# A decoder layer on one core: low parts of expert weights on VectorE, remainder rows by halves, second pass of two norms on VectorE

## The chip, the cores and the metric

The kernel runs on one core of one Trainium2 chip. The metric is device time in microseconds (us), the median of several executions. The engines are TensorE (PE; its weight loads are listed apart as PEld), VectorE (DVE), ScalarE (ACT), GpSimd (POOL) and SyncE (SP, which here only issues DMAs).

## The reference

One decoder layer over 1024 tokens of 1024 channels. Its first sublayer (sparse attention and RWKV-7 side by side) and the second (cross-attention) come before the part that is changed. The change touches the norm after the second sublayer, the mixture of experts, and the last norm:

```python
y = memory_cross_attention(x, mem, xq_w[l], xk_w[l], xv_w[l], xo_w[l])
x = layer_norm(DN_ALPHA * x + y, ln2_g[l], ln2_b[l])
y = grouped_moe(x, router_w, router_bias, moe_w_gate[l], moe_w_up[l], moe_w_down[l])
x = layer_norm(DN_ALPHA * x + y, ln3_g[l], ln3_b[l])
```

`grouped_moe` sends each token to 2 of 16 experts; an expert is `(silu(x @ w_gate) * (x @ w_up)) @ w_down` with a hidden width of 512, and its results are weighted and summed per token. With the reference's inputs, and the reference's own routing evaluated on them, the 16 experts get 123, 122, 118, 141, 118, 132, 142, 134, 129, 111, 138, 108, 127, 122, 123 and 160 tokens.

## The kernel before

Every f32 operand of a large product is split into a high part (rounded to fp32r by ScalarE) and a low part (the difference). A product is three matmuls, high by high, high by low, low by high (`Ctx.mm3`, lines 35 to 37).

**Second norm and routing.** `Xattn.out` makes one tile of 128 tokens at a time: TensorE's two halves, VectorE's residual add (line 1236), then `Norm.__call__`. A norm takes moments on VectorE (978, 979), `rs = (var + eps) ** -0.5` in two GpSimd instructions on 128x1 (980, 981), the first pass `(x - mean) * g` on VectorE (987), and the second pass `x * rs + b`, either as one VectorE instruction (992) or as a ScalarE multiply and a GpSimd add (989, 990). The list given as `pool_adds` says which tiles take the second way; the count starts at 1, so that `LN2P` of 0 to 7 means tiles 0 to 6. `Router.tile` then transposes the tile, forms logits, and after tiles 3, 6 and 7 `Router.route` finds experts and slots on VectorE (1338, 1341) and GpSimd scatters (row, gate) records into two lists in DRAM (1407). The first expert's tokens are picked by matmuls with a selection matrix (1417).

**Experts.** Each expert has room for 128 tokens (`CAP`, the "main" rows); the eight fullest, with expert 0 first, get 64 more (`REM`, the "remainder"). `rows` reads 128 list records, adds both lists, and makes two row numbers on GpSimd: the token to gather, and the row to add the result to, which for an empty slot is one of 128 spare rows behind the 1024. `gather` fetches rows of the normed x by an indirect DMA from GpSimd's queue (1551). For a remainder the 64 records are read twice, into both halves of the partitions, all 128 partitions gather whole rows, and half of every transpose is then dropped. High and low part of the remainder share one stationary operand of 128 columns, so that its results come out in two halves, both added by one indirect DMA each.

Weights come in pieces of 128x4x512 (six per expert); `parts` makes high and low of a piece in `CUT` = 4 steps: ScalarE casts (1528) and the difference is taken by GpSimd for the steps in `LOPOOL`, by VectorE otherwise (1529). `result` scales a result on ScalarE (1627) and adds its rows to `accd` in DRAM by an indirect DMA with accumulation (1632); each of these waits for the landing of the one before.

**End.** Before the last two experts are added, `tiles` loads `accd` tile by tile and norms it (`BYACT`: moments on ScalarE, 972 to 974; `ADDV`: second pass on VectorE, else ScalarE and GpSimd), and stores it. For the last two experts (`late`) the affected rows are gathered again, their results added (1629), normed, and scattered to the output (1635). `rest` handles experts with more than their room in a loop, which with these inputs runs no time.

The order of instructions on each engine is set when the program is built, by a scheduler over the whole program; engines issue in that order.

Of the kernel before, what the change touches and what calls it, by code (L numbers as in the profile page):

```python
# [7 lines left out]
F32 = mybir.dt.float32  # L8
F32R = mybir.dt.float32r
I32 = mybir.dt.int32  # L10
# [5 lines left out]
T, D = 1024, 1024  # L16
# [924 lines left out]

ALPHA = 2 ** 0.25
LN1P = ()
LN2P = (0, 1, 2, 3, 4, 5, 6, 7)
LN2A = ()
SQB = 2
EARLY = 4
# [291 lines left out]


NE, FF = 16, 512
CAP, REM = 128, 64
NREM = 8
FIXED = 1
# [1 line left out]
NSLOT = NE * REG  # L1246
NBLK = 15
LOOK = 4
BYACT, ADDV = (2, 3, 4, 5, 6), (0, 3, 5, 7)
NLAG = 1  # L1250
KINDS = ("raw", "hi", "lo")
NLST = 2
GROUPS = (4, 7, 8)
FIRST = (14, 6, 6, 6, 6, 6, 6, 7)
HOLD = 4
CUT, LOPOOL = 4, (2,)
LATE = 2


def host_consts5():  # L1260
    i = np.arange(128)
    rows = np.zeros((128, 8, 2, 4), np.float32)
    rows[:, :, :, 0] = (np.arange(8)[None, :] * 128 + i[:, None])[:, :, None]
    rows[:, :, :, 1] = 1
    e = np.arange(16)
    dum = (T + i).astype(np.float32)
    return {"c_upper": (i[:, None] < i[None, :]).astype(np.float32),
            "c_ones": np.ones((128, 128), np.float32),
            "c_e16": np.tile(np.concatenate([e - 16, REG * e]).astype(np.float32), (128, 1)),
            "c_rows": rows, "c_dum": np.stack([dum, -dum], 1),  # L1270
            "c_ii": np.tile(np.eye(64, dtype=np.float32), (2, 1)),
            "c_iota": np.tile(np.arange(128, dtype=np.float32), (128, 1)),
            "c_thr": np.tile((128 * np.arange(7)).astype(np.float32), (1, 16, 1)),
            "c_key": np.where(e < FIXED, 1e6 - e, 15 - e).astype(np.float32)[None],
            "c_er": np.stack([e, REG * e]).astype(np.float32)[None],
            "c_blk0": np.arange(NBLK).astype(np.float32)[None]}
# [195 lines left out]
class Experts:  # L1472
    def __init__(self, k, cst, p, pw, dp, router, x2d, out):
        self.out, self.held = out, 0
        self.k, self.r, self.x2d, self.ident = k, router, x2d, cst["ident"]
        nc = k.nc
        self.acc = dp.tile([T + 128, D], F32, name="accd")
        self.dum, self.ii = p.tile([128, 2], F32, name="dum"), pw.tile([128, 64], F32, name="ii")
        nc.sync.dma_start(self.dum, k.a["c_dum"])
        nc.sync.dma_start(self.ii, k.a["c_ii"])  # L1480
        nc.sync.dma_start(self.acc[T:T + 128, :].rearrange("p (a b) -> p a b", a=8), router.z[:, :128].unsqueeze(1).to_broadcast([128, 8, 128]))

        self.pre, self.at, self.done, self.seq = [], 0, [], []
        for n in range(NE + 1):
            self.seq += [(e, i) for e, i in ((n, 0), (n, 1), (n - 1, 4), (n - 1, 5), (n, 2), (n, 3)) if 0 <= e < NE]
        self.n, self.slots = {n: 0 for n in KINDS}, {n: [] for n in KINDS}
# [45 lines left out]
    def rows(self, pl, s0, tag, twice=False):  # L1532

        nc = self.k.nc
        l = pl.tile([128, NLST, 4], F32, tag="l" + tag, bufs=2, name="el")
        for i in range(NLST):
            src = self.r.lst[i][bass.ds(s0, 64 if twice else 128), :]
            nc.sync.dma_start(l[:, i, :], src.unsqueeze(0).to_broadcast([2, 64, 4]) if twice else src)
        f = pl.tile([128, 5], F32, tag="f" + tag, bufs=3, name="ef")
        ix = pl.tile([128, 2], I32, tag="ix" + tag, bufs=3, name="eix")  # L1540
        for i in range(1, NLST):
            nc.gpsimd.tensor_tensor(f[:, 0:4], l[:, 0] if i == 1 else f[:, 0:4], l[:, i], ALU.add)
        nc.gpsimd.tensor_copy(ix[:, 0:1], f[:, 0:1])
        nc.gpsimd.tensor_scalar(f[:, 4:5], f[:, 1:2], self.dum[:, 1:2], self.dum[:, 0:1], ALU.mult, ALU.add)
        nc.gpsimd.tensor_tensor(f[:, 4:5], f[:, 4:5], f[:, 0:1], ALU.add)
        nc.gpsimd.tensor_copy(ix[:, 1:2], f[:, 4:5])
        return ix, f[:, 2:3]

    def gather(self, px, ix, tag, src=None):
        xg = px.tile([128, D], F32, tag="xg" + tag, bufs=2 if tag == "m" else 1, name="exg")  # L1550
        self.k.nc.gpsimd.indirect_dma_start(out=xg, out_offset=None, in_=self.x2d if src is None else src, in_offset=bass.IndirectOffsetOnAxis(ap=ix[:, 0:1], axis=0))
        return xg

# [10 lines left out]
    def expert(self, px, ps, w, main, rem, first=None, late=False):  # L1564
# [14 lines left out]
        nc.vector.scalar_tensor_tensor(th, th, 1.0, o, ALU.add, ALU.mult)  # L1579
        if rem:  # L1580
            xr = px.tile([128, 8, 128], F32R, tag="exr", bufs=1, name="exr")
            for q in range(2):
                tp = self.turned(ps, rem[2], q).rearrange("p (c t) -> p c t", c=4)
                k.split(tp[:, :, 0:64], xr[:, 4 * q:4 * q + 4, 0:64], xr[:, 4 * q:4 * q + 4, 64:128])
            gr = px.tile([128, 2, 512], F32, tag="gr", bufs=1, name="egr")

        def more(i):
# [30 lines left out]
        def result(tag, x, mm):  # L1618
# [10 lines left out]
                    nc.vector.scalar_tensor_tensor(z[:, ds], o, x[1], z[:, ds], ALU.mult, ALU.add)  # L1629
            for r in ([slice(0, 128)] if tag == "m" else [slice(0, 64), slice(64, 128)]):  # L1630
                ix = x[0][0:r.stop - r.start, 1:2]
                nc.gpsimd.indirect_dma_start(out=self.acc, out_offset=bass.IndirectOffsetOnAxis(ap=ix, axis=0), in_=y[r, :], in_offset=None, compute_op=ALU.add)
            if late:
                self.ln(z)
                nc.gpsimd.indirect_dma_start(out=self.out, out_offset=bass.IndirectOffsetOnAxis(ap=x[0][:, 1:2], axis=0), in_=z, in_offset=None, bounds_check=T - 1, oob_is_err=False)
# [277 lines left out]
```

## Time and profile before

| | us |
|---|---|
| three runs | 1892.65, 1894.74, 1884.31 (median 1892.65) |
| profiled execution, its own time | 1896.58 |
| its span, first to last instruction | 1894.70 |
| mean granted TensorE clock | 0.959 |

The profile is of one execution, whose time lies 1.9 us above its span and 3.9 us above the median of the runs. Busy time is what an engine's instructions cover; a wait names what ended an engine's idle time. Times in the trace count from the start of the span.

### The profile page before, as it was taken

What the parts mean: (1) busy time and instruction counts of PE and PEld (TensorE: products, weight loads), DVE (VectorE), ACT (ScalarE), POOL (GpSimd) and SP (SyncE); (2) the same over time, 40 slices, a digit from 0 to 9 for tenths busy, and PEclk for the clock granted to TensorE, in tenths of its full rate; (3) what the DMA queues carried; (4) which work ended last, traced back from release to release, by engine and by line L of the source; (5) the groups of instructions that cost most, each with busy time, mean ns of one, the idle gap of its engine ahead of it and who ended that gap; (6) DMA issues with size and microseconds to landing.
All of it is one profiled execution on the core that took longest, in us unless ns stands there. A gap on an engine that the chain in (4) does not pass through costs nothing. (4 is left out here: it accounts for less than half of the span.)

```text
span 1894.7 us, 27396 instructions
## 1 busy us (share of the span) xinstructions
PE 1759.3 (93%) x9158; PEld 1433.4 (76%) x9158; DVE 1321.1 (70%) x2767; ACT 858.6 (45%) x1775; POOL 698.1 (37%) x780
## 2 busy tenths in 40 slices
PE   8999999999999899999999789999998999999991
PEld 6877777777687787888887577878787888877871
DVE  3225876888777621498987575546987788989876
ACT  4223313434332222298887441024414666667662
POOL 1123202221221121175747122100346576656556
PEclk9999989999999899999999899999989999999995
DMA  7363434444432226812101765133325999899984
GB/s 232 110 186 105 118 142 124 135 128 121 108 111 87 67 89 198 255 43 75 46 8 36 226 211 172 34 97 123 117 107 172 332 325 309 278 294 302 332 269 152
DMA packets 246143, 301.98 MB, mean 159 GB/s; under 512 B 54653, under 2 KB 142741, under 8 KB 245488
## 3 DMA queue, kind: packets, MB, share of 16 engines
q1 hardware_dynamic: 238016, 273.59, 44.4%
q0 software_dynamic: 7984, 26.62, 5.7%
q8 instruction: 73, 1.20, 0.3%
q14 instruction: 70, 0.57, 0.1%
HBM read 234.05 MB, written 70.98 MB: 161 GB/s over the span
## 5 line engine op out<-in xcount | busy, mean ns | idle before, releaser
L1529 DVE TENSOR_TENSOR wlo<-wraw,whi 128x512 fp32r<-128x512 f32 x288 | 281.1, 1026 | 26.1 <-ACT whi L1528 25.7
L35 PE MATMUL acc<-xh,wh 128*128 128x512 f32 (+1 forms) x656 | 273.6, 417 | 5.9 <-ACT wh L117 3.0
L36 PE MATMUL acc<-xl,wh 128*128 128x512 f32 (+1 forms) x656 | 267.1, 408 | 0.0
L37 PE MATMUL acc<-xh,wl 128*128 128x512 f32 (+1 forms) x656 | 266.6, 408 | 0.2 <-POOL wl L118 0.2
L1528 ACT CAST whi<-wraw 128x512 fp32r<-128x512 f32 x384 | 207.8, 623 | 35.4 <-PE eacc L1591 10.2
L118 POOL TENSOR_TENSOR wl<-wraw,wh 128x1024 fp32r<-128x1024 f32 (+1 forms) x41 | 100.8, 2459 | 308.6 <-ACT wh L117 259.2
L35 PEld LDWEIGHTS acc<-xh,wh 128*128 128x128 f32 (+1 forms) x656 | 125.1, 191 | 45.3 <-issue 8.0
L1529 POOL TENSOR_TENSOR wlo<-wraw,whi 128x512 fp32r<-128x512 f32 x96 | 138.8, 1482 | 46.4 <-ACT whi L1528 40.5
L37 PEld LDWEIGHTS acc<-xh,wl 128*128 128x128 f32 (+1 forms) x656 | 124.6, 190 | 33.7 <-issue 5.2
L36 PEld LDWEIGHTS acc<-xl,wh 128*128 128x128 f32 (+1 forms) x656 | 125.0, 191 | 29.8 <-issue 3.1
L851 DVE TENSOR_TENSOR tinv<-xinv,ln 128x248 f32<-128x248 f32 (+30 forms) x248 | 89.3, 360 | 40.6 <-DMA ln<-ld 15.6
L475 ACT ACTIVATE pp<-pp,nm 128x640 f32<-128x640 f32 (+7 forms) x128 | 94.3, 740 | 9.3 <-DVE nm L474 8.1
L28 DVE TENSOR_TENSOR pl<-ptp,ph 128x512 fp32r<-128x512 f32 x132 | 87.4, 685 | 12.0 <-ACT ph L28 11.3
L36 PE MATMUL eacc<-wlo,exh 128*128 128x512 f32 x240 | 94.2, 392 | 0.2 <-DVE wlo L1529 0.2
L35 PE MATMUL eacc<-whi,exh 128*128 128x512 f32 x240 | 94.2, 393 | 0.0
L37 PE MATMUL eacc<-whi,exl 128*128 128x512 f32 x240 | 94.2, 392 | 0.0
L480 POOL TENSOR_SCALAR pp<-pp,wgt 128x640 f32<-128x640 f32 (+7 forms) x128 | 88.4, 711 | 0.6
L852 DVE TENSOR_TENSOR xinv<-xinv,tinv 128x248 f32<-128x248 f32 (+30 forms) x248 | 84.0, 339 | 5.9
L980 POOL TENSOR_SCALAR lnrs<-lnmv 128x1 f32<-128x1 f32 x21 | 19.7, 936 | 180.5 <-DVE lnmv L979 172.6
L28 ACT CAST ph<-ptp 128x512 fp32r<-128x512 f32 x132 | 73.8, 583 | 16.9 <-PE ptp L534 16.1
L534 PE MATMUL ptp<-ident,pp 128*128 128x128 f32 x528 | 79.2, 276 | 0.4 <-DVE pl L28 0.2
L909 ACT COPY state<-rseq 64x64 f32<-64x64 f32 x128 | 26.8, 209 | 116.4 <-PE rseq L905 97.5
(502 smaller groups left out, 4542.9 us busy)
## 6 DMA issues: line engine op xcount, KB each, us to landing
wraw<-in_moe_w_up SPq DMA_DIRECT2D x32, 1024.0 KB
wraw<-in_moe_w_gate SPq DMA_DIRECT2D x32, 1024.0 KB
wraw<-in_moe_w_down SPq DMA_DIRECT2D x32, 1024.0 KB
wraw<-in_w_in SPq DMA_DIRECT2D x40, 512.0 KB
sm<-ev SPq DMA_DIRECT2D x32, 256.0 KB
sr<-ev SPq DMA_DIRECT2D x28, 256.0 KB
skew<-skew SPq DMA_DIRECT2D x1, 4608.0 KB
xraw<-in_x SPq DMA_DIRECT2D x8, 512.0 KB
```

What stands on the lines that cost most here:

```text
L28: x = nc.scalar.copy(hi, src), (nc.gpsimd if by_pool else nc.vector).tensor_tensor(lo, src, hi.bitcast(F32), ALU.subtract)
L35: nc.tensor.matmul(out, ah, bh, start=start, stop=False)
L36: nc.tensor.matmul(out, ah, bl, start=False, stop=False)
L37: nc.tensor.matmul(out, al, bh, start=False, stop=stop)
L118: nc.gpsimd.tensor_tensor(wl, raw, wh.bitcast(F32), ALU.subtract)
L475: nc.scalar.activation(pt[:, :n], pt[:, :n], AF.Exp, bias=nm, scale=-1.0, accum_out=sums[:, 0, i:i + 1])
L480: nc.gpsimd.tensor_scalar(st[br, i][:, :n], st[br, i][:, :n], w[:, 0, i:i + 1], 1.0, ALU.mult, ALU.mult)
L534: nc.tensor.transpose(tp[:, 128 * i:128 * i + 128], st[br, i][:, c0:c0 + 128], ident)
L851: nc.vector.tensor_tensor(tmp[:, :, :w], x[:, :, j:j + 1].to_broadcast([128, 8, w]), ln[:, j:j + 1, j + 1:].to_broadcast([128, 8, w]), ALU ...
L852: nc.vector.tensor_tensor(x[:, :, j + 1:], x[:, :, j + 1:], tmp[:, :, :w], ALU.subtract)
L1528: nc.scalar.copy(hi[:, cs], raw[:, cs])
L1529: (nc.gpsimd if i in LOPOOL else nc.vector).tensor_tensor(lo[:, cs], raw[:, cs], hi[:, cs].bitcast(F32), ALU.subtract)
```

## The change

Five things, all from the second norm on. (1) `LOPOOL` becomes empty: VectorE makes all low parts of the expert weights. (2) `LN2P` becomes empty and `ADDV` all eight tiles: the second pass of the second and last norm is VectorE's everywhere. (3) A remainder is gathered by halves: x is seen as 2048 half rows, the lower 64 partitions fetch the first half of their row (number 2r) and the upper 64 the second (2r + 1), one GpSimd instruction more makes the number, and four transposes and one split take the place of eight and two. (4) The adding DMA gets a bound, so that rows of empty slots are not written. (5) The row numbers lie in the same tile as the records, of which there are six per kind instead of three.

```diff
-LN2P = (0, 1, 2, 3, 4, 5, 6, 7)
+LN2P = ()
+NROWS = 6
-BYACT, ADDV = (2, 3, 4, 5, 6), (0, 3, 5, 7)
+BYACT, ADDV = (2, 3, 4, 5, 6), (0, 1, 2, 3, 4, 5, 6, 7)
-CUT, LOPOOL = 4, (2,)
+CUT, LOPOOL = 4, ()
-            "c_rows": rows, "c_dum": np.stack([dum, -dum], 1),
+            "c_rows": rows, "c_dum": np.stack([dum, -dum, (i >= 64).astype(np.float32)], 1),
...
-        f = pl.tile([128, 5], F32, tag="f" + tag, bufs=3, name="ef")
-        ix = pl.tile([128, 2], I32, tag="ix" + tag, bufs=3, name="eix")
+        f = pl.tile([128, 8], F32, tag="f" + tag, bufs=NROWS, name="ef")
+        ix = f[:, 6:8].bitcast(I32)
...
-        nc.gpsimd.tensor_copy(ix[:, 0:1], f[:, 0:1])
+        if twice:
+            nc.gpsimd.tensor_scalar(f[:, 5:6], f[:, 0:1], 2.0, self.dum[:, 2:3], ALU.mult, ALU.add)
+        nc.gpsimd.tensor_copy(ix[:, 0:1], f[:, 5:6] if twice else f[:, 0:1])
...
+        if tag == "r":
+            xg, src = xg[:, :D // 2], self.x2d.rearrange("t (h d) -> (t h) d", h=2)
...
-            for q in range(2):
-                tp = self.turned(ps, rem[2], q).rearrange("p (c t) -> p c t", c=4)
-                k.split(tp[:, :, 0:64], xr[:, 4 * q:4 * q + 4, 0:64], xr[:, 4 * q:4 * q + 4, 64:128])
+            tp = self.turned(ps, rem[2], 0).rearrange("p (c h t) -> p c h t", c=4, h=2)
+            x4 = xr.rearrange("p (h c) t -> p c h t", h=2)
+            k.split(tp, x4[:, :, :, 0:64], x4[:, :, :, 64:128])
...
-                nc.gpsimd.indirect_dma_start(..., compute_op=ALU.add)
+                nc.gpsimd.indirect_dma_start(..., compute_op=ALU.add, bounds_check=T - 1, oob_is_err=False)
```

How the instructions stand on an engine before and after, at three places (line numbers behind the changed ones are 1 to 6 higher in the changed kernel).

GpSimd among the first experts, from the last row numbers of the third expert on (`ef`, `eix`: records and row numbers; `exg`: gathered rows; `accd`: results). Before:

```order
L1551 DMA exg<-x2d,eix 128x1024
L1545 TENSOR_TENSOR ef<-ef 128x1
L1529 TENSOR_TENSOR wlo<-wraw,whi 128x512
L1546 CAST eix<-ef 128x1
L1529 TENSOR_TENSOR wlo<-wraw,whi 128x512 x8
L1632 DMA accd<-ey,eix 1152x1024
```

After:

```order
L1557 DMA exg<-x2d,ef 128x1024
L1549 TENSOR_TENSOR ef<-ef 128x1
L1550 CAST ef<-ef 128x1
L1638 DMA accd<-ey,ef 1152x1024
L1543 TENSOR_TENSOR ef<-el 128x4 x2
```

The nine subtractions shown, which stood ahead of the first result's adding DMA, are gone from the queue, and the row numbers of the next experts follow it at once.

VectorE at token tile 6 (`x_6`) of the second norm, beside the routing of tiles 0 to 3 (`gh`, `ms`, `oh`, `m`). Before:

```order
L979 BN_AGGR lnmv<-lnst 128x2
L1341 TENSOR_REDUCE m_13121<-ms 128x4
L987 SCALAR_TENSOR_TENSOR x_6_11297<-x_6_11297,lnmv,ln2g 128x1024
L1338 TENSOR_TENSOR oh_13131<-ms,m_13121 128x64
L1338 TENSOR_TENSOR oh_13131<-oh_13131,ce_11880 128x64
```

After:

```order
L979 BN_AGGR lnmv<-lnst 128x2
L1339 TENSOR_TENSOR gh<-ce_11880,m_13117 128x16
L987 SCALAR_TENSOR_TENSOR x_6_11297<-x_6_11297,lnmv,ln2g 128x1024
L1371 TENSOR_SCALAR gh<-gh 128x16
L1321 COPY rxt<-rtp 128x512
L992 SCALAR_TENSOR_TENSOR x_6_11297<-x_6_11297,lnrs,ln2b 128x1024
L1339 TENSOR_TENSOR ms<-ss,gh 128x64
```

The second pass now stands two places behind the first, ahead of the routing's next steps.

VectorE at the end, around the low part of the last expert's hidden values (`ehl`, for which TensorE waits); `wraw` are the tiles of the last norm, `exg` the rows of the last two experts. Before:

```order
L1629 SCALAR_TENSOR_TENSOR exg_17890<-eacc_17907,ef_17164,exg_17890 128x512
L28 TENSOR_TENSOR ehl_17963<-etp_17964,ehh_17962 128x512
L979 BN_AGGR lnmv_17845<-lnst_17847 128x2
L987 SCALAR_TENSOR_TENSOR wraw_17768<-wraw_17768,lnmv_17824,exgr_17758 128x1024
L978 BN_STATS lnst_17925<-exg_17890 128x6
L987 SCALAR_TENSOR_TENSOR wraw_17769<-wraw_17769,lnmv_17845,exgr_17758 128x1024
```

After:

```order
L1635 SCALAR_TENSOR_TENSOR exg_17867<-eacc_17884,ef_17146,exg_17867 128x512
L992 SCALAR_TENSOR_TENSOR wraw_17747<-wraw_17747,lnrs_17762,eexr_17740 128x1024
L28 TENSOR_TENSOR ehl_17942<-etp_17943,ehh_17941 128x512
L992 SCALAR_TENSOR_TENSOR wraw_17748<-wraw_17748,lnrs_17784,eexr_17740 128x1024
L978 BN_STATS lnst_17904<-exg_17867 128x6
L987 SCALAR_TENSOR_TENSOR wraw_17749<-wraw_17749,lnmv_17803,exgr_17739 128x1024
```

Second passes (992) of tiles that ScalarE and GpSimd finished before now stand on both sides of `ehl`.

## Rows read from the trace of the kernel before

**Rows 1.** The page: section 1 for TensorE (busy us, share of the span, instructions) and section 3 for the queue that the indirect DMAs of GpSimd use (packets, MB, share of 16 engines over the span).
```profile
PE 1759.3 (93%) x9158; PEld 1433.4 (76%) x9158; DVE 1321.1 (70%) x2767; ACT 858.6 (45%) x1775; POOL 698.1 (37%) x780
...
q0 software_dynamic: 7984, 26.62, 5.7%
```

**Rows 2.** Busy time by stretch, from the end of cross-attention to the end of the program: the stretch (us from the start of the span), its length, then busy us and instruction count of PE, PEld, DVE, ACT and POOL, granted TensorE clock, DMA share, GB/s.
```profile
1360.00:1430.00 70.00, 66.09 (x433) 61.73 (x434) 54.16 (x175) 13.51 (x24) 31.09 (x29) 0.88 0.25 91
1430.00:1473.00 43.00, 36.02 (x167) 28.66 (x166) 37.80 (x69) 24.40 (x49) 26.68 (x39) 0.92 0.66 230
1473.00:1835.50 362.50, 354.35 (x1690) 290.94 (x1689) 305.28 (x362) 246.59 (x473) 224.55 (x228) 1.00 0.95 302
1835.50:1872.00 36.50, 17.81 (x65) 12.81 (x63) 31.60 (x36) 19.50 (x32) 29.08 (x25) 0.78 0.69 244
1872.00:1894.70 22.70, 0.00 (x0) 0.00 (x0) 8.40 (x9) 0.00 (x0) 7.83 (x8) 0.50 0.37 111
```

**Rows 3.** Waits of TensorE from 1430 us to the end: who waited, for whom, us in total, times, longest.
```profile
PE etp L1558 <- DMA exg<-x2d,eix: 8.2, 3, 5.0
PE eacc L35 <- ACT ehh L28: 6.0, 2, 5.3
PE eacc L37 <- DVE ehl L28: 5.6, 2, 3.9
PE eacc L1639 <- DVE ehr L28: 2.7, 6, 0.9
PE eacc L1591 <- DVE exr L28: 2.1, 2, 1.7
...
PE eacc L36 <- DVE wlo L1529: 0.2, 1, 0.2
```

**Rows 4.** The low parts of the expert weights (line 1529): from the page the group on VectorE (busy us, mean ns | idle before it); both engines' instructions over the whole run (ns, least / median / longest); busy time of that line alone in the expert stretch (DVE, then POOL); and from the timeline three of them on VectorE beside two on GpSimd.
```profile
L1529 DVE TENSOR_TENSOR wlo<-wraw,whi 128x512 fp32r<-128x512 f32 x288 | 281.1, 1026 | 26.1 <-ACT whi L1528 25.7
...
L1529 DVE TENSOR_TENSOR wlo<-wraw,whi x288: 639/682/4751, 1363.6 to 1845.1; 128x512 fp32r<-128x512 f32 x144
...
L1529 POOL TENSOR_TENSOR wlo<-wraw,whi x96: 1261/1357/1861, 1364.7 to 1837.9; 128x512 fp32r<-128x512 f32 x96
...
1473.00:1835.50 362.50, 246.91 (x250) 121.24 (x84) 1.00 0.95 302
...
1364.84 3.98 DVE L1529 TENSOR_TENSOR wlo<-wraw,whi 128x512 fp32r<-128x512 f32 x3
...
1364.71 1.27 POOL L1529 TENSOR_TENSOR wlo<-wraw,whi 128x512 fp32r<-128x512 f32 x1 [9.66 <-ACT whi L1528]
1366.79 1.48 POOL L1529 TENSOR_TENSOR wlo<-wraw,whi 128x512 fp32r<-128x512 f32 x1 [0.80 <-ACT whi L1528]
```

**Rows 5.** Transposes and gathers at the start of the experts: from the chain that ended last, eight transposes at full clock; from the timeline of TensorE, eight of the remainder rows of the first expert; from the chain, the gather that they waited for (start, us from issue to landing).
```profile
1479.23 0.87 PE etp L1558 x8
...
1441.21 1.97 PE L1558 MATMUL etp<-ident,exg 128*128 128x128 f32 x8 [5.01 <-DMA exg<-x2d,eix]
...
1436.80 4.37 DMA exg<-x2d,eix
```

**Rows 6.** The timeline around the last row tiles of the second norm and the routing (start us, us, engine, line, operation, tiles, count, and in brackets the idle time before and what ended it): VectorE, then GpSimd, then TensorE.
```profile
1384.25 2.38 DVE L1347 TENSOR_SCALAR sg<-sg 128x64 f32<-128x64 f32 x1
...
1390.81 1.29 DVE L987 SCALAR_TENSOR_TENSOR x<-x,lnmv,ln2g 128x1024 f32<-128x1024 f32 x1
...
1394.79 1.76 DVE L1338 TENSOR_TENSOR oh<-ms,m 128x64 f32<-128x64 f32 x1
...
1373.80 0.22 POOL L980 TENSOR_SCALAR lnrs<-lnmv 128x1 f32<-128x1 f32 x1 [5.54 <-DVE lnmv L979]
...
1384.18 2.39 POOL L990 TENSOR_TENSOR x<-x,ln2b 128x1024 f32<-128x1024 f32 x1 [1.26 <-ACT x L989]
1390.86 1.31 POOL L980 TENSOR_SCALAR lnrs<-lnmv 128x1 f32<-128x1 f32 x1 [4.28 <-DVE m L1341]
...
1394.09 2.38 POOL L990 TENSOR_TENSOR x<-x,ln2b 128x1024 f32<-128x1024 f32 x1 [1.26 <-ACT x L989]
...
1413.02 0.58 PE L1385 MATMUL ra<-mm,cupper 128*128 128x16 f32 x2 [1.43 <-DVE tmp L1338]
```

**Rows 7.** The timeline of the end, columns as in Rows 6: VectorE, then GpSimd.
```profile
1839.04 1.29 DVE L978 BATCH_NORM_STATS2 lnst<-wraw 128x6 f32<-128x512 f32 x2 [6.24 <-DMA wraw<-accd]
...
1843.34 2.45 DVE L1529 TENSOR_TENSOR wlo<-wraw,whi 128x512 fp32r<-128x512 f32 x4
...
1862.07 4.61 DVE L987 SCALAR_TENSOR_TENSOR wraw<-wraw,lnmv,exgr 128x1024 f32<-128x1024 f32 x2
...
1870.55 3.36 DVE L987 SCALAR_TENSOR_TENSOR exg<-exg,lnmv,exgr 128x1024 f32<-128x1024 f32 x1
1873.84 1.40 DVE L1629 SCALAR_TENSOR_TENSOR exg<-eacc,ef,exg 128x512 f32<-128x512 f32 x2
...
1879.96 1.29 DVE L992 SCALAR_TENSOR_TENSOR exg<-exg,lnrs,eexr 128x1024 f32<-128x1024 f32 x1 [0.78 <-POOL lnrs L981]
...
1862.22 3.37 POOL L990 TENSOR_TENSOR wraw<-wraw,eexr 128x1024 f32<-128x1024 f32 x1
1865.76 1.85 POOL L1551 DMA_INDIRECT exg<-accd,eix  x1 [0.17 <-issue]
...
1883.04 1.08 POOL L1635 DMA_INDIRECT out<-exg,eix  x1 [3.11 <-DMA out<-exg,eix]
```

More of the change, by code (lines that the diff above doesn't have):

```diff
@@ L1477, in __init__ @@
         self.acc = dp.tile([T + 128, D], F32, name="accd")
-        self.dum, self.ii = p.tile([128, 2], F32, name="dum"), pw.tile([128, 64], F32, name="ii")
+        self.dum, self.ii = p.tile([128, 3], F32, name="dum"), pw.tile([128, 64], F32, name="ii")
         nc.sync.dma_start(self.dum, k.a["c_dum"])
@@ L1631, in result @@
                 ix = x[0][0:r.stop - r.start, 1:2]
-                nc.gpsimd.indirect_dma_start(out=self.acc, out_offset=bass.IndirectOffsetOnAxis(ap=ix, axis=0), in_=y[r, :], in_offset=None, compute_op=ALU.add)
+                nc.gpsimd.indirect_dma_start(out=self.acc, out_offset=bass.IndirectOffsetOnAxis(ap=ix, axis=0), in_=y[r, :], in_offset=None, compute_op=ALU.add, bounds_check=T - 1, oob_is_err=False)
             if late:
```

## The prediction

> **What bounds the kernel now.** I read the page first: TensorE is busy for 93% of the span [rows 1], so the time is TensorE's work plus its idle time, and another engine counts only where TensorE or the last chain waits for it. Cutting the second half by stages [rows 2] shows three different limits. From 1473 to 1835.5 us, the experts, TensorE is busy 354.35 of 362.5 us at granted clock 1.00: 8 us of idle time are all there is to win besides its own instructions. VectorE is busy 305 us there and the DMA engines 0.95, so both are near the edge without being it. From 1360 to 1473 (second norm, routing, first expert) TensorE idles 4 + 7 us at a mean clock of 0.88 to 0.92, and after 1835.5 the chain runs through VectorE (31.6 of 36.5 us) and GpSimd (29.1), with TensorE half idle at 0.78.
>
> The waits of TensorE [rows 3] say for whom: 8.2 us for gathered rows, of which 5.0 in one piece, about 12 for the hidden values of an expert (ehh, ehl), 4.8 for splits of a remainder (ehr, exr), and only 0.2 for the low parts of weights. So moving the low parts is worth nothing by itself: what counts is what it does to VectorE's queue.
>
> **The low parts.** 96 of 384 go from GpSimd to VectorE. The group's mean on VectorE is 1026 ns, but its median is 682 and its longest 4751 [rows 4]: two populations. On the timeline three on VectorE take 3.98 us while GpSimd makes two of its own [rows 4]; four in a row with GpSimd elsewhere take 2.45, 0.61 each [rows 7]. I take 0.61 to 0.68 as the price once GpSimd makes none. In the expert stretch VectorE spends 246.9 of its 305.3 us on 250 low parts and 58.4 on the rest [rows 2, 4]. After: 250 + 84 = 334 at 0.61 to 0.68 are 204 to 227 us, with the rest 262 to 286. VectorE gets 19 to 43 us lighter although it does a third more pieces. ScalarE's casts are unchanged. Direct gain on TensorE: 0, as the 0.2 us of waits says; the cover is TensorE's own 354 us.
>
> **Remainders by halves.** Eight experts give up four transposes each. At the first expert eight took 1.97 us, so four are 1.0; later eight took 0.87, so 28 are 28 x 0.109 = 3.05 [rows 5]. This is TensorE's own time in a stretch that it bounds: **-4.0** (bounds -3.5 to -4.5). The split of eight half tiles becomes one of four whole ones, and GpSimd makes one more small instruction ahead of each remainder's gather, some 0.2 to 1.3 us by its like on 128x1 [rows 6]. The gather moves half the bytes. At the first expert it took 4.37 us from issue to landing [rows 5]; how much of that is bytes the rows don't tell, so between -1.1 (a quarter, an estimate) and +1.3 (the extra instruction at its longest). I take 0.
>
> **Empty slots.** The 16 x 128 + 8 x 64 = 2560 slots hold 2048 tokens; by the counts of the inputs 80 main slots and 432 remainder slots are empty, the latter written twice: 944 rows of 4 KB, 3.9 MB. With 2.1 MB fewer gathered that is 6.0 of the 26.6 MB that the indirect queue moves in 5.7% of 16 engines' span, 108 us [rows 1]: an estimated 24 us of all engines, out of 0.95 x 362.5 = 344. TensorE does not wait for weights, so no direct gain. But gathers and adding DMAs share these engines, and GpSimd, rid of 121 us of subtractions in the stretch [rows 4], issues them sooner; six record tiles per kind instead of three take away a wait too. Of the 8 us of idle time I give back **-3.5** (bounds 0 and -8): the gather waits beyond the first (3.2) and a little of the splits, which stand behind shorter low parts on VectorE.
>
> **Second norm and routing.** Tile 6 is the last whose second pass moves (tile 7's was VectorE's already). Its rs was ready when ScalarE began, at 1392.86, and GpSimd's add ended at 1394.09 + 2.38 = 1396.47 [rows 6]. VectorE's pass is 1.28 to 1.29 long [rows 7] and stands two places behind the first pass, which ended near 1392.1 [rows 6]; with rs some 0.7 later it ends about 1394.2, 2.3 us earlier. Against that VectorE gets three passes (tiles 4 to 6, 3.8 us) and two low parts (1.2). In return two tiny routing instructions that lasted 2.38 and 1.76 us, each until GpSimd's add was over (1384.25 + 2.38 against 1384.18 + 2.39, 1394.79 + 1.76 against 1396.47) shrink to a fraction, and three low parts lose 2.1: about 5.7 off, 5.0 on. Queued behind these are the routing steps for which TensorE waits at 1413.02 [rows 6]. I take the 2.3 less a little: **-2.2** (bounds -5, both effects in full, and +5, the added work alone). Tiles 0 to 3 get four passes, 5.1 us, beside cross-attention's matmuls of the second half; I cost them at nothing, and at 5.1 if that cover is gone.
>
> **The end.** Four second passes (5.1 us) and two low parts (1.2) come to VectorE. Off go GpSimd's adds, beside which a first pass took 3.36 instead of 1.29 and two took 4.61 [rows 6, 7]: 4.1 us back. The gather for the last expert was issued at 1865.76, just as an add of 3.37 ended (1862.22 + 3.37), and the addition for which it was fetched started at 1873.84, just as the lengthened pass ended (1870.55 + 3.36) [rows 7]. Both releases together let that addition start up to 5 us earlier. But in the new order the first and second pass for the last but one expert stand behind it, 2.6 us, and the last scatter waits for that expert's rows to land (3.11 us at 1883.04) [rows 7]. 5.0 - 2.6: **-2.4** (bounds -6 and +5).
>
> **Sum.** -4.0 - 3.5 - 2.2 - 2.4 = -12.1 us. The profiled execution took 1896.58, so it would take 1884.5; the runs' median, 1892.65, is 3.9 lower, and so I forecast 1880.6, rounded to 1881. A difference of 0.5%, 9.5 us, is about what can be told from no change here.
>
> **The rivals.**
> - *Hidden anyway.* The waits move to the next late thing (the split after the transposes, ScalarE's casts), and only TensorE's own 4.0 us show: 1888.6. For it: the largest single wait, 5.0 us at the first expert, follows a chain of list scatters that the change doesn't shorten.
> - *GpSimd's small steps held up.* Each norm's rs is made by GpSimd on 128x1. Such a step took 0.22 us alone and 1.31 when it began with VectorE's first pass (1390.86 beside 1390.81) [rows 6]; second passes are of the same kind, so on the four norms on the path (tiles 6 and 7, the last two experts) 4 x 1.1 = 4.4 come on top: -7.7, 1885.0. Against it: the first passes already do this, and the trace has it in its times.
> - *The passes are exposed.* VectorE is in order, and all eleven moved passes, 11 x 1.28 = 14.1 us, come onto the path: +14.1 - 4.0 = +10.1, 1902.8. It ends as slower only from 13.5 us exposed, nearly all of them; the shortened neighbours speak against it.
> - *Low parts are slow on VectorE themselves.* At 1026 ns, 334 pieces and the rest are 401 us, 38.7 over the stretch: about 1927. VectorE becomes the bound from (355 - 58) / 334 = 0.89 us each; the median of 682 excludes it nearly.
> - *More.* All waits of [rows 3] vanish, 24.8 us: 1863.8.
>
> The second rival is also a rule of the Trainium skill, SBUF — State Buffer, section "Who interferes with whom": a VectorE instruction with two SBUF inputs and a GpSimd instruction that reads SBUF exclude each other, and the loser waits for the whole instruction. By that rule every moved pass can hold up a step of GpSimd, which would leave the 7.7 us above. The trace agrees for GpSimd's adds, subtractions and small steps [rows 4, 6].
>
> **Chances.** Forecast 0.50, hidden 0.25, small steps 0.10, passes exposed 0.08, low parts slow 0.02, more 0.05. Faster than 1883.2: 0.50 + 0.05; within 0.5%: 0.25 + 0.10; slower: 0.10. The range leaves out the two slow rivals and most of the largest gain: 1867 to 1894.
>
> **What would show it.** The group of low parts on VectorE at x384 with a mean near 685 ns and a sum near 262 us; VectorE below 290 us in the expert stretch; TensorE's transposes of gathered rows 32 fewer; the gather waits beyond the first gone; the indirect queue some 6 MB lighter; no ScalarE multiply or GpSimd add in the norms from the second on; the last addition near 1868 to 1870 on the scale of this trace. The forecast is wrong if first or second passes at the end are followed by idle time that waits for rs, if the last but one expert's scatter lands later than now, or if the list scatters of the routing start later than before.

## The result and the profile after

The changed kernel took 1871.8 us (median of four runs, 1868.5 to 1875.7) beside 1893.0 for the kernel before: a ratio of 0.990 (of the means; the medians lie 21 us apart), 95% interval 0.986 to 0.993, or 19 us off with 12 to 26 as bounds. The forecast was 1881 in a range of 1867 to 1894. So direction and range held; the size was forecast too small, and most of what follows is on why.

The page of the changed kernel: section 1 (engines), section 3 (GpSimd's indirect queue) and the group of low parts on VectorE, which answer to [rows 1, 4].

```profile
PE 1744.0 (93%) x9126; PEld 1423.5 (76%) x9126; DVE 1277.4 (68%) x2866; ACT 845.5 (45%) x1756; POOL 535.9 (29%) x681
...
q0 software_dynamic: 7472, 20.67, 4.5%
...
L1530 DVE TENSOR_TENSOR wlo<-wraw,whi 128x512 fp32r<-128x512 f32 x384 | 237.4, 683 | 30.0 <-ACT whi L1529 30.0
```

384 low parts at a mean of 683 ns where 288 had 1026, 32 instructions fewer on TensorE, 6.0 MB fewer in the queue: the change does what it says. Its waits of TensorE from 1420 us on, which answer to [rows 3]:

```profile
PE etp L1564 <- DMA exg<-x2d,ef: 6.7, 1, 6.7
PE eacc L37 <- DVE ehl L28: 6.4, 1, 6.4
PE eacc L1645 <- DVE ehr L28: 5.1, 7, 1.1
PE eacc L35 <- ACT ehh L28: 3.1, 2, 2.4
PE eacc L1597 <- DVE exr L28: 1.4, 1, 1.4
```

Only the first expert's gather is still waited for (6.7, before 5.0); the later ones are gone.

To compare kernels whose stages start at different times I cut each trace at three events of its own: the first query matmul of the second sublayer (`xacc`; up to it TensorE, VectorE, ScalarE and GpSimd issue the same instructions in the same order in all kernels here), and ScalarE's tanh of the gate of the second expert and of the last (number fifteen when counted from 0, as the expectations below do). I call the stretches between them **B** (second norm, routing, first expert), **C** (the experts) and **D** (the end); what comes ahead is **A**. The columns are those of [rows 2]. The kernel before:

```profile
1240.50:1466.20 225.70, 209.28 (x1136) 176.08 (x1134) 167.40 (x439) 85.60 (x184) 72.62 (x82) 0.94 0.36 125
1466.20:1831.50 365.30, 356.23 (x1702) 292.86 (x1703) 311.39 (x371) 245.57 (x471) 224.79 (x228) 1.00 0.96 306
1831.50:1894.70 63.20, 21.08 (x80) 15.31 (x78) 40.69 (x45) 23.50 (x39) 38.75 (x34) 0.69 0.56 185
```

The changed kernel:

```profile
1232.50:1458.00 225.50, 209.49 (x1143) 176.68 (x1141) 168.37 (x460) 78.33 (x175) 38.83 (x67) 0.93 0.37 128
1458.00:1812.40 354.40, 349.30 (x1666) 287.87 (x1666) 265.79 (x443) 243.63 (x464) 109.51 (x150) 1.00 0.90 298
1812.40:1870.30 57.90, 21.46 (x81) 15.88 (x78) 40.45 (x51) 19.57 (x35) 24.59 (x26) 0.69 0.57 195
```

The two traces differ by 24.4 us: 8.0 in A, 0.2 in B, 10.9 in C, 5.3 in D. Eight microseconds ahead of any changed instruction can't be the change's. That was the first thing to settle.

### The profile page after: what moved, and what is told of

It is laid out like the page before. It is cut to its first block, busy times and chain, and to the rows that moved or that the text cites. A ratio compares the mean times of both kernels' runs of the same rounds, so it can differ in the third digit from the quotient of the medians.

```text
span 1870.3 us, 27135 instructions
## 1 busy us (share of the span) xinstructions
PE 1744.0 (93%) x9126; PEld 1423.5 (76%) x9126; DVE 1277.4 (68%) x2866; ACT 845.5 (45%) x1756; POOL 535.9 (29%) x681
## 5 line engine op out<-in xcount | busy, mean ns | idle before, releaser
L1530 DVE TENSOR_TENSOR wlo<-wraw,whi 128x512 fp32r<-128x512 f32 x384 | 237.4, 683 | 30.0 <-ACT whi L1529 30.0
L1638 POOL DMA_INDIRECT accd<-ey,ef x32 | 52.6, 1642 | 141.6 <-ACT ey L1633 60.1
```

The lines of the kernel that those rows point to most:

```text
L1530: (nc.gpsimd if i in LOPOOL else nc.vector).tensor_tensor(lo[:, cs], raw[:, cs], hi[:, cs].bitcast(F32), ALU.subtract)
```

## The experiments

Twelve kernels, in three groups of four; the kernels of a group ran on one chip and beside the same runs of the kernel before, so ratios are safe and times of different groups are not.

| kernel | ratio to before (95%) | B | C | D |
|---|---|---|---|---|
| before, the trace shown | | 225.7 | 365.3 | 63.2 |
| `c_before`: before again | 1.0012 (0.9992 to 1.0032) | 236.1 | 365.5 | 63.9 |
| `c_lo`: + low parts | 1.0158 (1.0136 to 1.0180) | 236.5 | 383.0 | 67.8 |
| `c_half`: + halves | 1.0057 (1.0036 to 1.0079) | 230.9 | 375.1 | 66.2 |
| `c_norm`: + second passes | 1.0037 (1.0021 to 1.0054) | 230.9 | 373.0 | 61.4 |
| `c_rows`: + six tiles | 1.0102 (1.0068 to 1.0136) | 229.5 | 388.3 | 63.9 |
| `c_lorows`: + low parts, six tiles | 1.0004 (0.9981 to 1.0027) | 232.8 | 357.4 | 68.7 |
| changed | 0.9898 (0.9862 to 0.9934) | 225.5 | 354.4 | 57.9 |
| `u_rows`: changed, three tiles | 0.9958 (0.9937 to 0.9980) | 232.9 | 360.7 | 61.2 |
| `u_lo`: changed, old low parts | 1.0049 (1.0027 to 1.0071) | 231.2 | 379.2 | 58.4 |
| `u_half`: changed, no halves | 0.9925 (0.9902 to 0.9949) | 228.3 | 359.6 | 59.8 |
| `u_norm`: changed, old second passes | 0.9977 (0.9961 to 0.9993) | 240.2 | 356.6 | 61.4 |
| `u_bound`: changed, no bound | 0.9941 (0.9921 to 0.9961) | 230.1 | 354.3 | 61.3 |
| `u_act8`: changed, all moments on ScalarE | 0.9913 (0.9893 to 0.9934) | 234.5 | 354.2 | 55.0 |

**The kernel before, again (`c_before`).** No edit.

> The kernel before, unchanged, run and profiled again. The two traces shown differ by 8.0 us already at the first query matmul of the second sublayer (1240.5 and 1232.5 us), up to which TensorE issues the same instructions in the same order. If that is variation between executions, this profile puts that matmul somewhere between 1232 and 1250 with nothing changed, and the time from it to the end stays near the 654.2 us of the trace before. If the change itself moved it (by its early DMAs), the matmul stays within 1 us of 1240.5. The ratio of times is 1.000 either way.

```profile
1230.50:1466.60 236.10, 215.69 (x1137) 182.00 (x1135) 167.55 (x439) 85.37 (x184) 72.06 (x82) 0.91 0.34 120
1466.60:1832.10 365.50, 355.99 (x1702) 292.88 (x1703) 303.70 (x371) 245.66 (x471) 222.60 (x228) 1.00 0.95 306
1832.10:1896.00 63.90, 23.94 (x81) 17.50 (x78) 40.71 (x45) 23.54 (x39) 38.70 (x34) 0.69 0.55 183
```

The event came at 1230.5, 10.0 us earlier with nothing changed, and B took 10.4 longer at a granted clock of 0.91 against 0.94; C and D agree to 0.2 and 0.7. So, by this one repeat, the lengths of A and B tell nothing below 10 us, C and D of one kernel come back within 1 us, and the 8.0 us of A are no more than variation. TensorE's idle time in B (its length less TensorE's busy time) moves less: 16.4 us in the kernel before, 20.4 here. From here on I argue from C and D, from this idle time, and from the ratios.

**Low parts alone (`c_lo`).**

```diff
-CUT, LOPOOL = 4, (2,)
+CUT, LOPOOL = 4, ()
```

> Only the low parts move from GpSimd to VectorE; all else as before. My prediction's theory: the low parts' mean falls from 1026 to about 685 ns, the experts' waits give back 3.5 us and the routing and the end a little, 4 to 7 us in all (ratio 0.996 to 0.998). Rival, shared access: what GpSimd's subtractions held up was worth more than the waits in the trace say, most of the gain of the whole change comes from here, 10 to 16 us (ratio 0.992 to 0.995). Rival, hidden anyway: 0 to 2 us (0.999 to 1.000), since TensorE waited 0.2 us for low parts.

30 us slower: all three theories were wrong. VectorE did get lighter (268.5 us in C, before 311.4), but TensorE waited for gathers. C, and the waits of TensorE in it:

```profile
1469.80:1852.80 383.00, 361.67 (x1715) 298.38 (x1714) 268.52 (x451) 246.61 (x474) 109.17 (x144) 0.96 0.89 288
```

```profile
PE etp L1558 <- DMA exg<-x2d,eix: 19.1, 6, 5.8
```

Why a gather is late is in GpSimd's timeline, here ahead of one of them:

```profile
1602.74 0.18 POOL L1543 CAST eix<-ef 128x1 int32<-128x1 f32 x1 [8.13 <-DMA accd<-ey,eix]
...
1603.49 1.05 POOL L1551 DMA_INDIRECT exg<-x2d,eix  x1 [0.44 <-POOL eix L1546]
```

The cast writes a tile of row numbers (`eix`, three per kind), and the adding DMA of an earlier expert still reads that tile: 8.13 us until it has landed, with the gather behind the cast. In C these casts wait 72.4 us in all; in the kernel before 30.0, hidden between subtractions. This gave a new theory, the ring of three tiles. In B TensorE waits for gathers too, 13.2 us against 5.0 in the kernel before; that has another reason, shown under `c_lorows`.

**Halves alone (`c_half`).** The gather by halves, the row number for it and the one split, as in the change's diff, with three tiles and `eix` as before.

> Only the remainders are gathered by halves (four transposes and one split in place of eight and two, one small GpSimd instruction more); all else as before. My prediction's theory: 4.0 us of TensorE's own time and nothing else, ratio 0.998; a first remainder gather of 3.3 to 5.7 us from issue to landing, against 4.4. Rival, hidden: TensorE waits for the next late thing instead, 0 to 1 us (1.000). Rival, the shorter gather and split also free waits: 7 to 9 us (0.995).

0.6% slower, outside all three. Gathers are waited for 13.6 us in C, in six pieces, the longest 2.9. It is not the ring's waits that grew (casts wait 14.0 us for adding DMAs, less than before); at 1603.90 us, for one, the gather is issued behind low parts that GpSimd still makes, and TensorE has its rows only at 1612.19. Which of the new order's steps makes them late was not tried.

**Second passes alone (`c_norm`).**

```diff
-LN2P = (0, 1, 2, 3, 4, 5, 6, 7)
+LN2P = ()
-BYACT, ADDV = (2, 3, 4, 5, 6), (0, 3, 5, 7)
+BYACT, ADDV = (2, 3, 4, 5, 6), (0, 1, 2, 3, 4, 5, 6, 7)
```

> Only the second passes of the second and last norm move to VectorE; GpSimd keeps a quarter of the low parts. My prediction's theory: 2.2 us at the routing and 2.4 at the end, 4.6 in all, less where GpSimd's low parts still hold VectorE up: 0 to 5 us (ratio 0.997 to 1.000). Rival, the passes are exposed: 3 to 14 us slower (1.002 to 1.007), with VectorE never idle at the end. Rival, most of the gain of the whole change is the end's: 8 to 12 us faster (0.994 to 0.996).

0.4% slower, in the range of the second theory, but not in its way. D is 1.8 us shorter (2.4 was forecast), so the passes were not exposed there; C is 7.7 longer, with 8.6 us of gather waits, although in C all four engines issue in the order of the kernel before (GpSimd has one small step more at its start). So the kernel before can lose several microseconds in C by the times at which it gets there. How a norm ahead of the experts brings this about stays open.

**Six tiles alone (`c_rows`).** The parts of the diff with `NROWS`, `f` and `ix`.

> The kernel before with room for six experts' row numbers (records and row numbers in one tile, six of them per kind), nothing else. New theory, the ring of three: in the kernel before, ten casts of row numbers on GpSimd wait 30.0 us between 1470 and 1850 us for the landing of an adding DMA that still reads the third last tile, with the next gather queued behind them. With six tiles these waits are gone, TensorE's gather waits in the expert stretch fall from 3 to 4 us to under 1, and with the clock that they cost the time falls by 3 to 8 us (ratio 0.996 to 0.998). Rival, contention: GpSimd's subtractions are the hold-up, the gathers stay as late and the ratio is 1.000. Rival, order: every change of order costs this kernel, as the three parts alone did, 1.003 to 1.010.

The gather waits went, as the ring says: none is left in C. Yet it is 1.0% slower, and something else is waited for. C, its largest wait, VectorE's low parts over the run (ns, least, median, longest), then the timeline of VectorE and GpSimd ahead of one such wait:

```profile
1458.60:1846.90 388.30, 363.35 (x1702) 298.62 (x1703) 321.74 (x371) 245.18 (x470) 211.99 (x227) 0.97 0.91 289
```

```profile
PE eacc L37 <- DVE ehl L28: 19.5, 6, 5.6
```

```profile
L1529 DVE TENSOR_TENSOR wlo<-wraw,whi x288: 639/681/7770, 1352.9 to 1861.3; 128x512 fp32r<-128x512 f32 x144
```

```profile
1702.35 10.07 DVE L1529 TENSOR_TENSOR wlo<-wraw,whi 128x512 fp32r<-128x512 f32 x4
1712.95 0.68 DVE L28 TENSOR_TENSOR ehl<-etp,ehh 128x512 fp32r<-128x512 f32 x1
...
1704.50 6.77 POOL L1529 TENSOR_TENSOR wlo<-wraw,whi 128x512 fp32r<-128x512 f32 x5
```

GpSimd, no longer stopped by the ring, makes five subtractions in a row, from 1704.50 to 1711.27. One low part on VectorE, begun at 1704.06 and 0.68 long elsewhere, lasts 7.77 us, until they are over; the low part of the hidden values (`ehl`) stands behind it, and TensorE waits 5.2 us. So the two engines do exclude each other, and what the low part waits for here is not one instruction but the whole run of them; each of the seven runs of three to five subtractions in this trace holds one low part to its end. Right behind TensorE's wait, at 1713.70 us, the granted clock is 0.50, and the wait costs more than its idle time:

```profile
1713.70:1718.00 4.30, 4.30 (x10) 3.43 (x11) 4.30 (x8) 0.00 (x0) 0.00 (x0) 0.50 1.05 396
```

**Low parts and six tiles (`c_lorows`).** Both edits.

> The kernel before with the low parts on VectorE and room for six row numbers; no halves, second passes as before. Theory of the ring: the low parts alone took 30 us because GpSimd, with nothing else to do, ran ahead into casts that waited 72.4 us for adding DMAs; with six tiles all of that goes and VectorE's lighter queue shows: the time between the second and the fifteenth expert's gates falls from 383.0 to 355 to 360 us, ratio 0.990 to 0.995 against the kernel before. Rival: the low parts themselves hold TensorE up (VectorE's order), the ratio stays above 1.010. Rival, the halves are needed too: 0.998 to 1.005.

C is 357.4, as the ring's theory expected: 7.9 us shorter than before, where the two parts alone made it 17.7 and 23.0 longer.

```profile
1465.20:1822.60 357.40, 354.50 (x1714) 293.18 (x1713) 267.70 (x451) 245.25 (x474) 100.39 (x144) 1.00 0.96 309
```

But the ratio is 1.000. D is 5.5 us longer than in the kernel before, which the runs here explain only in part (`u_bound` and `u_norm`, below), and in B TensorE idles 24.7 us, 13.2 of them for gathers. The timeline of GpSimd, VectorE and TensorE in B has

```profile
1430.55 4.93 POOL L1546 CAST ef<-ef 128x1 int32<-128x1 f32 x1
...
1436.42 1.02 POOL L1551 DMA_INDIRECT exg<-x2d,ef  x1 [0.22 <-POOL ef L1544]
...
1430.54 4.89 DVE L1529 TENSOR_TENSOR wlo<-wraw,whi 128x512 fp32r<-128x512 f32 x8
...
1444.28 1.08 PE L1558 MATMUL etp<-ident,exg 128*128 128x128 f32 x4 [8.60 <-DMA exg<-x2d,ef]
```

The same exclusion the other way round: eight low parts in a row on VectorE, 4.89 us, hold a cast of 128 numbers, 0.18 us elsewhere, for 4.93. The gather behind it is 5 us late, and TensorE waits 8.6. But this is the exception. In the same trace another run of eight low parts lets GpSimd's small steps in between:

```profile
1527.68 4.90 DVE L1529 TENSOR_TENSOR wlo<-wraw,whi 128x512 fp32r<-128x512 f32 x8
...
1528.91 1.31 POOL L1542 TENSOR_TENSOR ef<-el 128x4 f32<-128x4 f32 x2 [4.64 <-DMA el<-lst]
1530.17 0.65 POOL L1543 CAST ef<-ef 128x1 int32<-128x1 f32 x1
```

Each of the three steps takes 0.6 to 0.7 us, about the time of one low part. Every trace has about 150 such steps (on 128x1 or 128x4) after 1360 us. One of them lasts over 2.5 us in `c_lo` (4.95), here (4.93), in `u_norm` (4.65) and in `c_norm` (3.15), and none in the other ten traces. What decides between the two is open.

**The change with three tiles (`u_rows`).**

```diff
-NROWS = 6
+NROWS = 3
```

> The changed kernel with three tiles for row numbers instead of six, all else as changed. Theory of the ring: GpSimd's casts wait for adding DMAs again, the gathers are late by 1 to 6 us each, and most of the gain is lost or more: 1885 to 1915 us, ratio 0.997 to 1.013 against the kernel before. My prediction's theory, in which six tiles were a small part of 3.5 us: 1873 to 1876 us, ratio 0.990 to 0.992.

0.9958, just under the ring's range and above the forecast's; C is 6.3 us longer, and GpSimd's row numbers wait for adding DMAs again:

```profile
POOL ef L1543 <- DMA accd<-ey,ef: 74.5, 11, 7.6
```

**The change with a quarter of the low parts on GpSimd (`u_lo`).** `LOPOOL` is `(2,)` again.

> The changed kernel with a quarter of the low parts back on GpSimd, all else as changed. If shared access is what the low parts cost (the group's mean back at about 1000 ns, VectorE 20 to 40 us fuller in the expert stretch, GpSimd's small steps held up), 5 to 12 us of the gain go: ratio 0.992 to 0.996. If the ring is the whole of it, the ratio stays at 0.990 although the low parts' mean is back at 1000 ns. If moving the low parts was harmful in itself, as the run of that part alone suggests, it falls below 0.986.

1.0049, a larger loss than any theory had: slower than the kernel before. C is 24.8 us longer than the changed kernel's, with no gather waited for; VectorE is busy 320.8 us, its longest low part 5.38.

```profile
1469.30:1848.50 379.20, 358.46 (x1675) 293.25 (x1675) 320.78 (x364) 244.31 (x465) 213.60 (x235) 0.98 0.88 282
```

**The change without halves (`u_half`).** Whole rows, eight transposes and two splits again.

> The changed kernel with the remainders gathered whole again (eight transposes and two splits each), all else as changed. My prediction's term: 4.0 us lost, 1876 us, ratio 0.992, with the time between the second and the fifteenth expert's gates 2.7 us longer than 354.4. If the shorter gather also counts at the first experts, where the run with low parts and six tiles alone waited 13.2 us for gathers and the changed kernel 6.7, 8 to 12 us are lost: 0.994 to 0.996.

0.9925, as forecast (0.992), though its interval overlaps that of the changed kernel. C is 5.2 us longer, and by more than was forecast for its 24 transposes (2.6 us at 0.109), but not through them: all 5.2 lie ahead of the third expert's gate. Of these 1.7 are no loss: in the changed kernel 15 small transposes of the first remainder (`etq`, 0.112 us each) fall ahead of C's start. The rest goes with one wait of 2.1 us for the low part of the remainder's hidden values (`ehr`) and a stretch at granted clock 0.50 behind it. From the third gate to the last one the changed kernel and this one take the same time:

```profile
1486.97:1812.44 325.47, 320.37 (x1534) 264.16 (x1533) 246.51 (x410) 225.66 (x431) 97.82 (x135) 1.00 0.90 294
```

```profile
1493.33:1818.67 325.34, 322.89 (x1558) 266.71 (x1557) 246.89 (x416) 226.03 (x437) 94.34 (x129) 1.00 0.90 297
```

The 2.5 us that TensorE is busy less in the changed kernel it is idle more. Its timeline shows where, between an expert's last product and its remainder's (again the changed kernel first):

```profile
1645.31 1.04 PE L1564 MATMUL etp<-ident,exg 128*128 128x128 f32 x8
1647.01 0.50 PE L1645 MATMUL eacc<-whi,ehr 128*128 128x512 f32 x1 [0.66 <-DVE ehr L28]
```

```profile
1651.67 1.47 PE L1559 MATMUL etp<-ident,exg 128*128 128x128 f32 x12
1653.36 0.50 PE L1640 MATMUL eacc<-whi,ehr 128*128 128x512 f32 x1 [0.22 <-DVE ehr L28]
```

Eight transposes and a wait of 0.66 us, or twelve and 0.22: 1.70 and 1.69. ScalarE's cast for `ehr` stands behind its scaling of the result that TensorE has just finished, VectorE's difference behind that cast, and the transposes were what TensorE did meanwhile.

**The change with the old second passes (`u_norm`).** `LN2P` and `ADDV` as before.

> The changed kernel with the second passes of both norms as before (ScalarE multiply and GpSimd add where before had them), all else as changed. My prediction's terms: 2.2 us at the routing and 2.4 at the end are lost, 4.6 in all, ratio 0.992. If the norms carry most of what low parts and six tiles alone do not explain (that run stands at 1.0004, the changed kernel at 0.990), 10 to 16 us are lost, ratio 0.995 to 0.998, and the last addition comes 15 to 20 us later than 1846. If the passes on VectorE only made its queue at the end longer (it is busy 31.0 of 31 us there), the ratio falls below 0.988.

0.9977: 15 us of the gain gone, the second theory's number, but not by its mechanism. D is 3.5 us longer; C's 2.2 are no loss, since six transposes and the 15 of `etq` fall behind its start here. B is 240.2, with 28.8 us of it idle (16.0 in the changed kernel), and there, as in `c_lorows`, it is a step of GpSimd held by a run of low parts (it began at 1433.98, a run of eight at 1433.68), and a gather behind it:

```profile
1433.98 4.65 POOL L1543 TENSOR_TENSOR ef<-el 128x4 f32<-128x4 f32 x1 [0.70 <-DMA el<-lst]
...
1448.21 1.94 PE L1564 MATMUL etp<-ident,exg 128*128 128x128 f32 x8 [12.10 <-DMA exg<-x2d,ef]
```

As far as this trace shows, the second passes matter less for what they cost than for the order that comes of them at the first expert: in the changed kernel the second expert's transposes stand behind the first's remainder on TensorE, and its gather isn't waited for. All three kernels with the low parts on VectorE and the old second passes (`c_lo`, `c_lorows` and this one) have such a held step, and none of the five with the new ones.

**The change without the bound (`u_bound`).** `bounds_check` is taken off the adding DMA.

> The changed kernel with the rows of empty slots written again (the adding DMA without its bound), all else as changed; TensorE and GpSimd issue in the same order as in the changed kernel. My prediction's term: the 944 rows, 3.9 MB, cost no time of their own, 1872 us, ratio 0.990, with only the indirect queue 3.9 MB heavier. If the adding DMAs' landings are what is left on the path, each remainder's is longer by some us and 3 to 8 us are lost: 0.991 to 0.994.

0.9941, at the upper end of the second theory's range, and its interval touches the changed kernel's. The trace has C at 354.3, the same to 0.1; D is 3.4 longer, B 4.6, A 3.7. A, and B up to the first adding DMA, hold nothing that the bound touches. D's 3.4 us are the bound's. VectorE's first moments of the last norm stand ahead of the last expert's gate product (`eth`) in its order, and wait for rows of `accd` that are loaded once the last adding DMA ahead of them has landed; the changed kernel, then this one:

```profile
1815.27 1.29 DVE L978 BATCH_NORM_STATS2 lnst<-wraw 128x6 f32<-128x512 f32 x2 [1.52 <-DMA wraw<-accd]
```

```profile
1827.06 1.29 DVE L978 BATCH_NORM_STATS2 lnst<-wraw 128x6 f32<-128x512 f32 x2 [5.16 <-DMA wraw<-accd]
```

From the issue of the last but one of these adding DMAs to the moments it takes 13.0 to 14.0 us in all eight kernels without the bound, and 9.8 to 10.8 in the five with it that make these moments on VectorE. In B some 8 us stand in rows of TensorE like these, among the matmuls that pick the first expert's tokens:

```profile
1418.53 0.38 PE L1418 MATMUL first<-sel,x 128*128 128x128 f32 x2 [0.94 <-issue]
1419.94 0.60 PE L1418 MATMUL first<-sel,x 128*128 128x128 f32 x2 [1.03 <-issue]
```

Two matmuls every 1.4 us, with nothing that the profile shows to wait for. Such rows are in all twelve profiles of this section (1.3 to 4.6 us of waits), that of the kernel before among them, and in neither of the two shown at first. What they are is open. The changed kernel was not run in this group, so that its 0.9898 and this 0.9941 don't tell the bound's part; the 3.4 us of D do.

**All moments on ScalarE (`u_act8`).**

```diff
-BYACT, ADDV = (2, 3, 4, 5, 6), (0, 1, 2, 3, 4, 5, 6, 7)
+BYACT, ADDV = (0, 1, 2, 3, 4, 5, 6, 7), (0, 1, 2, 3, 4, 5, 6, 7)
```

> A try at a better version: the changed kernel with the moments of all eight tiles of the last norm on ScalarE (five in the changed kernel). Between 1819 and 1850 us VectorE is busy 31.0 of 31 us and ScalarE 13.8; TensorE waits 6.4 us for the low part of the last expert's hidden values, which stands behind passes on VectorE. Three tiles' moments, 3 x 1.5 us, leave VectorE's queue: if that queue is what sets the end, 3 to 5 us faster than the changed kernel (ratio 0.987 to 0.988). If ScalarE's moments, 2.6 us a tile, then hold up its cast ahead of that low part, 0 to 4 us slower (0.990 to 0.992).

D is 55.0, 2.9 us shorter than the changed kernel's; the wait that it aimed at fell from 6.4 us to

```profile
PE eacc L37 <- DVE ehl L28: 1.6, 1, 1.6
```

Another wait, for VectorE's gate product (`eth`), rose from 0.2 to 2.9. Its ratio, 0.9913, can't be told from the changed kernel's, which was not measured beside it. Beside `u_bound`, which ran with it, it is 5.2 us faster (1878.1 and 1883.4), of which 3.4 are the bound's. Likely better by 2 to 3 us, and not shown to be.

## Why the forecast was right in sign and too small

**Low parts.** Forecast: about 685 ns each, 262 us in sum, VectorE at 262 to 286 us in the expert stretch, nothing gained directly. Measured: 683, and 265.8 in C (before 311.4). Right. Alone, though, the edit costs 30 us.

**Waits among the experts: the step that was mis-sized.** -3.5 (0 to -8) was forecast. C fell by 10.9, or 9.2 without the 1.7 us of `etq`, and the transposes have no part in it (*Halves*, below). Most of it comes from low parts and six tiles alone: from the third gate to the last the kernel before takes 333.0 us, `c_lorows` 325.1 and the changed kernel 325.5. So the term measured some 9 us, past its bound of 8. Two things were wrong in it. First, the six tiles were a clause, "take away a wait too". They are one half of a pair: undone, they cost 6.3 us of C and, by the ratios, about 11 us. I had read TensorE's waits and not GpSimd's, where the row was:

```profile
POOL eix L1543 <- DMA accd<-ey,eix: 30.0, 10, 4.0
```

Second, I took the idle time, 8 us, as all that could be won. After a wait the matmuls run at a lower granted clock and count as busy: `c_lo` and `c_lorows` issue the same 1714 or so instructions in C, busy for 361.7 us at 0.96 and for 354.5 at 1.00, and behind a wait in `c_rows` it stood at 0.50. 18.4 us more idle time came with 7.2 us more busy time, 40 per cent on top.

**Parts do not add.** The sum treated the edits as separate terms. Four of them alone make the kernel slower. Low parts and six tiles are the clearest: C changes by +17.7, +23.0 and, together, -7.9. GpSimd's subtractions filled the time in which its casts waited, and those waits kept the subtractions from running in a row against VectorE (runs of three or more: three in the kernel before, seven in `c_rows`). Take away one, and the other is exposed.

**Halves: the step that failed.** -4.0 was forecast, as TensorE's own time in a stretch that it bounds. The 32 transposes are gone, but of their time nothing is won from the third gate on: 320.4 us busy and 5.1 idle in the changed kernel stand against 322.9 and 2.5 in `u_half`. Those transposes had covered a wait for `ehr`. Eight of the 32 fall in B, where they can't be read, and the ratios of `u_half` and the changed kernel overlap. That the sum came as near as it did is in part luck: about as much came from the bound, for which nothing was forecast.

**Empty slots.** No direct gain was forecast. The queue is 6.0 MB lighter and C doesn't change, as it said, but D is 3.4 us shorter (`u_bound`). The row was at hand: VectorE's idle time of 6.24 us at 1839.04 for a tile of `accd` [rows 7]. I hadn't asked what that load waited for.

**Second norm and routing.** -2.2 was forecast and isn't to be seen: the first list scatter comes 167.7 us after the event `xacc` in the kernel before and 167.4 after the change. B varies by 10 us in any case, so the term is neither shown nor excluded. The gather that I had kept at 0 is waited for 6.7 us instead of 5.0 (2.0 in `u_bound`, which issues in the same order).

**The end.** -2.4 was forecast; D fell by 5.3, 3.4 by the bound and 1.9 by the rest. The terms stand in GpSimd's gather and VectorE's rows of the changed kernel:

```profile
1846.10 0.74 DVE L1635 SCALAR_TENSOR_TENSOR exg<-eacc,ef,exg 128x512 f32<-128x512 f32 x1
...
1856.72 1.28 DVE L992 SCALAR_TENSOR_TENSOR exg<-exg,lnrs,eexr 128x1024 f32<-128x1024 f32 x1 [2.94 <-POOL lnrs L981]
...
1837.83 1.05 POOL L1557 DMA_INDIRECT exg<-accd,ef  x1 [5.41 <-DVE wraw L992]
```

Counted from the last gate, the addition starts 33.7 us behind it, before 42.3: 8.6 earlier, where 5.0 was forecast. Of these, 3.5 are there already at the last `eth` (12.0 us behind the gate, before 15.5) and are the bound's; 5.1 remain. From the addition to the last second pass it takes 10.6 us, before 6.1 [rows 7]: 4.5 given back to the passes that now stand behind it, where 2.6 was forecast; the rest of D is 1.2 shorter (13.5, before 14.7). So the first term was right and the second too small, and without the bound the net is near the forecast's.

**The rivals.** *Hidden anyway* and *passes exposed* fell: C and D both got shorter. Something was hidden, but it was the transposes' time, the part that *hidden anyway* had kept. *Low parts slow on VectorE* fell with 683 ns. *GpSimd's small steps held up* has the right mechanism at the wrong place: not second passes against a norm's rs, but runs of low parts against the row numbers, with up to 4.9 us instead of 1.1, and in `c_lo`, `c_lorows` and `u_norm`, not in the changed kernel, where no such step lasts over 2.5. The Trainium skill (SBUF — State Buffer, section "Who interferes with whom") says that the loser waits for the whole instruction of the other; the rows above agree that one waits for the other (0.65 us for a cast of 0.18), and some go further: the loser waited for a run of five or eight.

What I can account for in the changed kernel is thus some 9 us in C and 5 in D, 14 of a measured 19 (12 to 26). The rest lies in A and B, where the kernel before differs from itself by as much.

## What to carry to other kernels

Look at the waits of the helper engine too: a queue that is stopped by a small ring of tiles may be the only thing that keeps it from running over its neighbour, so remove the ring and the contention together. Before counting work taken off the busiest engine as time won, look for the wait that this work covers: 2.5 us of transposes came back as 2.6 us of waits. Price a wait of TensorE above its idle time; here it cost 1.4 times as much. And run the kernel before a second time and cut the traces at events, not at times, before reading a microsecond into any stage.

## What the runs showed of the hardware that I had not expected

A run of subtractions on GpSimd can hold one of VectorE to the end of the run: 7.77 us for 0.68 (five in a row). A run on VectorE can hold a small step of GpSimd in the same way, 4.93 us for 0.18 (eight low parts), but did so in three traces only, once in each; mostly such a step got in behind one low part, at 0.65. An execution of the same program can be 10 us faster in its first two thirds and 10 slower behind: granted clock 0.94 and 0.91 in B, with the times of the whole 1.3 us apart. And TensorE can be slowed among small matmuls (two every 1.4 us, for some 8 us) by something that the profile shows only as "issue".
